# A decoder layer on one core: input loads held in program order, activation sums made in small steps, one input transposed two half-steps later

## The chip, the cores and the metric

The kernel runs on one core of a Trainium2 chip. The time is that of one execution on the device in microseconds (us), as the median of several runs. The five engines of the core take part as follows: TensorE multiplies and transposes (PE in the profile, its weight loads PEld), ScalarE (ACT) and VectorE (DVE) prepare operands and finish results, SyncE (SP) starts nearly all transfers, and GpSimd (POOL) does next to nothing here.

## The reference

One layer on x of 256 rows by 2048 columns, in float32:

- h = x + half FFN 1, where a half FFN is `0.5 * ((silu(gate) * up) @ w_down)` with `gate, up = split(rmsnorm(x) @ w_gate_up)`. The hidden width is 5632, so w_gate_up is 2048 x 11264 and w_down 5632 x 2048.
- Three mixers on rmsnorm(h) @ w_in (causal window means, attention with a forget gate, attention to 256 memory rows), each gated; their sum goes through w_out (2048 x 2048) and is added to h.
- A second half FFN with its own norm and weights is added to that; the sum is the output.

## The kernel before

**Products.** Every float32 operand is cut into a high part and the remainder; a product is three matmuls (high by high, high weight-remainder, remainder by high), each of 128 x 128 by 512 columns. ScalarE writes the high part of a weight tile (`wh`), VectorE the remainder (`wl`). The activations are the stationary side: a page of the transposed input holds two slices of 128 input columns for both halves of the rows, as high part and remainder. `to_lhs_part` (L189) makes such a page: four transposes on TensorE (L197), then ScalarE (L186) and VectorE (L187) cut what stands in PSUM.

**Two kinds of groups.** `mm_group` (L318) is the ordinary one: 512 output columns, all of the input. It loads weights in pieces of four slices (1 MB, L327) into a ring of three `raw` buffers, cuts half a piece at a time (L339, L340), and issues twelve matmuls for it (L346). Such a half is called a half-step here. `pair_group` (L245) does two blocks of 512 columns together, in eight units of two slices each. In units 0 to 2 seven products take the place of eight: VectorE forms sums of weights (`ta` L286, `tb` L291 and L292; their cut parts are `hah`, `hal`, `hbh`, `hbl`), and the stationary side needs sums of activation blocks, called `form`, one page for each of the three units. `form_page` (L212) makes one: VectorE adds high part and remainder (L216), forms four sums of 128 x 128 per slice (L218 to L221) and the remainder (L224), ScalarE the high part (L223). Units run in the order 3, 0, 4, 1, 5, 2, 6, 7.

**The sides of the work.** A queue `side` holds small jobs: transposes of a page (`prepare` for x, `to_lhs` for later inputs), loads of small parameters, empty steps (`pause`). `tick` takes one job from it behind each half-step of an ordinary group, and in a pair group only in the units behind the last one with seven products. The first group of FFN 1, `pa`, is an ordinary one with finer first loads (one slice, one, two, then four) and a hook: `before(k0)` (L503) loads the next columns of x ahead of the half-steps that need them. Behind it come `pb` (again ordinary) and ten pair groups, then w_down. FFN 2 has the same shape. In `ffn`, three calls of `form_page` stand between `pb` and the first pair group (L458); in the w_out section they stand between its two ordinary groups and its pair group (L902); the mixers have theirs in `side` already (L605). `residual`'s `cb` adds a result to the old stream and puts its transposes into `side`; thus w_out's columns 0 to 1023 become pages of x2 first, and columns 1024 to 2047, which the pair group makes, become its last four pages.

**What sets the order.** The program is written in Python, but `TileContext(schedule_with_timeline_sim=True)` (L945) arranges each engine's instructions anew by a timeline that it estimates itself. Only what is wrapped in `keep_in_program_order` keeps its place. Each engine runs its list strictly in that order, so an instruction that waits holds up all behind it. Transfers that SP starts share one queue.

Of the kernel before, what the change touches and what calls it, by code (L numbers as in the profile page):

```python
# [32 lines left out]
def hybrid_layer(  # L33
# [27 lines left out]
    nc = tc.nc  # L61
# [9 lines left out]
    side = deque()  # L71
    pause = [lambda: None]
# [10 lines left out]
    def page(shape, dtype, name):  # L83
        return pp.tile([P, *shape], dtype, tag="p", name=name)

    def pages(n, shape, dtype, name):
        return [page(shape, dtype, name) for _ in range(n)]

    def bank(name):
        return mp.tile([P, 512], F32, tag="m", name=name)  # L90

    def temp(shape, name, dtype=F32):
        return tp.tile([P, *shape], dtype, tag="t", name=name)
# [5 lines left out]
    xv = x[0].rearrange("(t p) d -> p t d", p=P)  # L99
    xc = pages(4, [T, 512], F32, "xc")  # L100

    def load_x(c0, n):
        nc.sync.dma_start(out=xc[c0 // 512][:, :, c0 % 512 : c0 % 512 + n], in_=xv[:, :, c0 : c0 + n])

    load_x(0, 256)
    rows0 = cp.tile([16, P], F32, name="rows0")
# [6 lines left out]
    for _ in range(2):  # L113
# [12 lines left out]
        out=tri, in_=tri, pattern=[[1, S]], compare_op=ALU.is_ge, fill=0.0, base=0, channel_multiplier=-1  # L126
# [4 lines left out]
        out=mask, in_=mask, pattern=[[-1, P]], compare_op=ALU.is_ge, fill=MASKED, base=0, channel_multiplier=1  # L131
# [77 lines left out]
    def lhs_of(tiles):  # L209
        return lambda k, part, t: tiles[k // 2][:, k % 2, part, t * P : (t + 1) * P]  # L210

    def form_page(forms, tiles, j):  # L212

        xp = tiles[j]
        v, f = temp([2, S], "fv"), temp([4, P], "ff")
        nc.vector.tensor_tensor(v, xp[:, :, 0, :].bitcast(F32), xp[:, :, 1, :].bitcast(F32), ALU.add)  # L216
        a12, a22, a11, a21 = (v[:, kk, t * P : (t + 1) * P] for kk in range(2) for t in range(T))
        nc.vector.tensor_tensor(f[:, 0, :], a21, a22, ALU.subtract)  # L218
        nc.vector.tensor_tensor(f[:, 1, :], f[:, 0, :], a11, ALU.subtract)
        nc.vector.tensor_tensor(f[:, 2, :], a11, a21, ALU.subtract)  # L220
        nc.vector.tensor_tensor(f[:, 3, :], f[:, 1, :], a12, ALU.add)  # L221
        dst = page([2, 4, P], F32R, "form")
        nc.scalar.activation(dst[:, 0, :, :], f, AF.Copy)  # L223
        nc.vector.tensor_tensor(dst[:, 1, :, :], f, dst[:, 0, :, :].bitcast(F32), ALU.subtract)  # L224
        forms.append(dst)
# [92 lines left out]
    def mm_group(w, c0, kt, lhs, cols=((0, 512),), before=None, need=None):  # L318

        ncol = sum(n for _, n in cols)  # L320
        per, half = 2048 // ncol, 1024 // ncol
        ps = [[bank("mm") for _ in cols] for _ in range(T)]
        cuts = [0, 1, 2, *range(4, kt + 1, per)] if before else [*range(0, kt, per), kt]
        for k0, k1 in zip(cuts, cuts[1:]):
            nk = k1 - k0
            raw = wp.tile([P, per, ncol], F32, tag="raw", name="raw")
            nc.sync.dma_start(  # L327
                out=raw[:, :nk, :],
                in_=w[k0 * P : (k0 + nk) * P, c0 : c0 + ncol].rearrange("(k p) c -> p k c", p=P),
            )  # L330
            if before:
                before(k0)
            if need:
                need(k0)
            for h0 in range(0, nk, half):
                nh = min(half, nk - h0)
                wh, wl = (b.rearrange("p (k c) -> p k c", c=ncol) for b in parts(half * ncol))
                rv, hv, lv = raw[:, h0 : h0 + nh, :], wh[:, :nh, :], wl[:, :nh, :]
                nc.scalar.activation(hv, rv, AF.Copy)  # L339
                nc.vector.tensor_tensor(lv, rv, hv.bitcast(F32), ALU.subtract)  # L340
                for t in range(T):
                    for kk in range(nh):
                        k = k0 + h0 + kk
                        for i, (o, n) in enumerate(cols):
                            for q, (part, wt) in enumerate(((0, wh), (0, wl), (1, wh))):
                                nc.tensor.matmul(  # L346
                                    ps[t][i][:, :n],
                                    lhs(k, part, t),
                                    wt[:, kk, o : o + n],
                                    start=k == 0 and q == 0,  # L350
                                    stop=k == kt - 1 and q == 2,
                                )
                tick()
        return ps
# [5 lines left out]
    def row_rstd(ss, name):  # L360
        r = st.tile([P, T], F32, tag="rr", name=name + "r")
        nc.vector.tensor_reduce(r, ss, axis=AX.X, op=ALU.add)
        return rsqrt(r, T, 1.0 / D, name)

    def sums(acc, terms, n):

        return [[acc[t, n]] + ([terms[t, n]] if terms else []) for t in range(T)]
# [34 lines left out]

        return cb, tiles, rs, Stream([kept[c].rearrange("p (t n) -> p t n", t=T) for c in range(4)])

    def ffn(lx, xt, rs, wgu, wd, stream, cb, before=None):

        hid, forms, flat = [], [], {}
        hdram = dp.tile([NFC - 1, P, 4 * S], F32, tag="hd", name="hd", bufs=2)
        rh = st.tile([P, T], F32, tag="rh", name="rh")

# [44 lines left out]
        pb = mm_group(wgu, FF, KD, lx)  # L455
        hd = gated(0, [pa[t][0] for t in range(T)], [pb[t][0] for t in range(T)])
        side.extend(put(0, hd))
        for j in range(3):  # L458
            form_page(forms, xt, j)
        for c in range(1, NFC):  # L460
            if c == NFC - 1:
                side.extend(put_last)
# [35 lines left out]
    tiles0, rs0 = [], []  # L498
# [16 lines left out]
    def row_sums(cs):  # L515
        for c in cs:
            for t in range(T):
                tc.keep_in_program_order(sumsq(ss0, t, c, xc[c][:, t, :]))
# [3 lines left out]
    for c in range(1, 4):  # L522
        side.append(lambda c=c: prepare(c, 0))
        side.append(lambda c=c: prepare(c, 1))
    side.append(lambda: row_sums(range(4)) or rs0.append(row_rstd(ss0, "x0")))
    side.append(small_loads)
    side.extend(pause * 6 + [small_cols])
    s0 = Stream([xv[:, :, c * 512 : (c + 1) * 512] for c in range(4)])
    cb, x1, rs, s1 = residual(s0, G_MIX, "x1", wait=3)
    lx = lhs_of(x1)  # L530
    ffn(lhs_of(tiles0), tiles0, rs0, ffn1_w_gate_up[0], ffn1_w_down[0], s0, cb, before=before)


    def head_norm(buf, nh, name):
# [67 lines left out]
                )  # L602

    forms1 = []
    side.extend(lambda j=j: form_page(forms1, x1, j) for j in range(3))  # L605
    side.append(load_mem)
    side.extend(pause)
    for c in range(4):
# [239 lines left out]
    mg = []  # L848
# [46 lines left out]

    cb, x2, rs, s2 = residual(s1, G_FFN2, "x2")
    lg = lhs_of(mg)
    for c in range(2):
        s1.load(c)
        ps = mm_group(w_out[0], c * 512, KD, lg)  # L900
        cb(c, [[ps[t][0]] for t in range(T)])
    formsg = []  # L902
    for j in range(3):
        form_page(formsg, mg, j)
    for c in range(2, 4):
        s1.load(c)
    po, terms = pair_group(w_out[0], 1024, 1536, lg, formsg, MIXED)
    for n in range(2):
        cb(2 + n, sums(po, terms, n))


    def store(c, ps):
# [1 line left out]
        for t in range(T):  # L914
            nc.sync.dma_start(out=out[0, t * P : (t + 1) * P, c * 512 : (c + 1) * 512], in_=o[:, t, :])

    ffn(lhs_of(x2), x2, rs, ffn2_w_gate_up[0], ffn2_w_down[0], s2, store)


# [30 lines left out]
```

## Time and profile before

| | |
|---|---|
| median of 3 runs | 2164.21 us (2162.13 to 2168.88) |
| the profiled execution | 2164.95 us, its span 2163.2 us |
| granted TensorE clock, mean | 0.997 of full speed |
| PE busy | 2142.4 us (99%), 9770 matmuls and transposes |
| PEld busy | 1764.5 us (82%) |
| DVE busy | 1572.2 us (73%) |
| ACT busy | 1136.0 us (53%) |
| DMA | 444.63 MB, mean 206 GB/s |

Busy time counts a matmul from its issue to its modelled end, and neighbours overlap; so 99% does not say that matmuls follow each other as closely as they can. How closely they do is read from a run of equal matmuls: its length over their number. The span is what the engines' records cover; the execution is 1.75 us longer.

### The profile page before, as it was taken

The numbers are of one execution on the slowest core, as the hardware profiler recorded it, in microseconds if no ns is written. First come the engines' busy times: TensorE is split into PE (matmuls) and PEld (weight loads), VectorE is DVE, ScalarE is ACT, GpSimd is POOL, SyncE is SP. The second block draws the span as 40 slices with busy tenths as digits, with TensorE's granted clock in tenths as the row PEclk, the third lists the DMA queues.
The fourth block names the chain that finished last, engine by engine and source line by source line (L and its number), as shares of the span: only waits on it lengthen the run. The fifth ranks groups of instructions, "written<-read, shape, count | busy, mean of one in ns | idle before, by whom it ended". The sixth has DMA issues, their size and how long they took to land.

```text
span 2163.2 us, 25670 instructions
## 1 busy us (share of the span) xinstructions
PE 2142.4 (99%) x9770; PEld 1764.5 (82%) x9770; DVE 1572.2 (73%) x1959; ACT 1136.0 (53%) x1412; POOL 3.5 (0%) x24
## 2 busy tenths in 40 slices
PE   8999999999999999999999999999999999999999
PEld 5888888888888888887788888878788888888887
DVE  4799889887554678657645777687989889984443
ACT  5455555556444465555644555455555555563332
POOL 0000000000000000000000000000000000000000
PEclk8999999999999999999999999999999999999999
DMA  6566666668666655754455656565666666686663
GB/s 215 175 220 219 213 206 212 215 212 304 212 205 207 236 182 158 242 172 149 144 194 192 196 180 217 193 222 183 211 217 215 220 207 214 205 311 233 204 200 112
DMA packets 219680, 444.63 MB, mean 206 GB/s; under 512 B 10831, under 2 KB 11941, under 8 KB 219557
## 3 DMA queue, kind: packets, MB, share of 16 engines
q1 hardware_dynamic: 219264, 442.95, 61.8%
q8 instruction: 76, 1.25, 0.2%
q14 instruction: 48, 0.39, 0.0%
q10 hardware_dynamic: 292, 0.05, 0.0%
HBM read 426.16 MB, written 16.79 MB: 205 GB/s over the span
## 4 chain that ended last, share of the span: by engine, by line
PE 94%; DVE 2%; DMA 2%; ACT 1%; issue 0%; SPq 0%; ACTq 0%
PE mm L346 48%; PE mm L241 42%; DMA raw<-in_ffn_w_gate_up_dram 2%; DVE wl L236 1%; PE hid L422 1%; ACT wh L235 0%; PE x L197 0%; DVE hal L236 0%; DMA xc<-in_x_dram 0%; PE fpt L829 0%; DMA raw<-in_w_out_dram 0%; PE fav L839 0%; ACT wh L339 0%; DVE tb L291 0%; DVE form L224 0%
## 5 line engine op out<-in xcount | busy, mean ns | idle before, releaser
L340 DVE TENSOR_TENSOR wl<-raw,wh 128x1024 fp32r<-128x1024 f32 (+2 forms) x393 | 471.0, 1200 | 405.8 <-ACT wh L339 405.0
L339 ACT ACTIVATE wh<-raw 128x1024 fp32r<-128x1024 f32 (+2 forms) x393 | 408.2, 1040 | 508.8 <-PE mm L346 447.9
L241 PE MATMUL mm<-wh,x 128*128 128x512 f32 x2116 | 655.0, 391 | 0.0
L235 ACT ACTIVATE wh<-raw 128x1024 fp32r<-128x1024 f32 (+1 forms) x384 | 374.4, 979 | 371.8 <-PE mm L241 188.2
L236 DVE TENSOR_TENSOR wl<-raw,wh 128x1024 fp32r<-128x1024 f32 (+1 forms) x384 | 424.6, 1118 | 101.3 <-ACT wh L235 99.7
L241 PEld LDWEIGHTS mm<-wh,x 128*128 128x128 f32 x2116 | 394.5, 188 | 80.7 <-ACT wh L235 0.3
L346 PE MATMUL mm<-wh,hid 128*128 128x512 f32 x1408 | 435.4, 390 | 0.0
L241 PE MATMUL mm<-wl,x 128*128 128x512 f32 x1058 | 408.2, 390 | 0.0
L346 PE MATMUL mm<-wh,x 128*128 128x512 f32 (+1 forms) x1216 | 375.6, 386 | 9.5 <-ACT x L186 8.1
L346 PEld LDWEIGHTS mm<-wh,hid 128*128 128x128 f32 x1408 | 264.3, 188 | 54.5
L346 PE MATMUL mm<-wl,hid 128*128 128x512 f32 x704 | 274.0, 389 | 0.0
L346 PEld LDWEIGHTS mm<-wh,x 128*128 128x128 f32 x1216 | 225.3, 189 | 58.1 <-ACT x L186 10.2
L241 PEld LDWEIGHTS mm<-wl,x 128*128 128x128 f32 x1058 | 198.6, 188 | 41.8
L346 PE MATMUL mm<-wl,x 128*128 128x512 f32 (+1 forms) x608 | 232.1, 382 | 0.0
L346 PEld LDWEIGHTS mm<-wl,hid 128*128 128x128 f32 x704 | 132.2, 188 | 27.4
L346 PEld LDWEIGHTS mm<-wl,x 128*128 128x128 f32 x608 | 115.2, 189 | 20.7 <-issue 0.3
L235 ACT ACTIVATE hbh<-tb 128x1024 fp32r<-128x1024 f32 x72 | 75.8, 1053 | 35.5 <-DVE tb L292 35.4
L286 DVE TENSOR_TENSOR ta<-raw 128x1024 f32<-128x1024 f32 x72 | 87.6, 1217 | 8.0 <-DMA raw<-in_ffn_w_gate_up_dram 7.0
L236 DVE TENSOR_TENSOR hbl<-tb,hbh 128x1024 fp32r<-128x1024 f32 x72 | 87.7, 1218 | 6.8 <-ACT hbh L235 6.8
L236 DVE TENSOR_TENSOR hal<-ta,hah 128x1024 fp32r<-128x1024 f32 x72 | 87.7, 1218 | 0.8 <-ACT hah L235 0.8
L241 PE MATMUL mm<-hah,form 128*128 128x512 f32 x288 | 86.0, 389 | 0.2 <-ACT hah L235 0.2
L235 ACT ACTIVATE hah<-ta 128x1024 fp32r<-128x1024 f32 x72 | 75.7, 1052 | 19.2 <-DVE ta L286 19.1
(319 smaller groups left out, 1923.2 us busy)
## 6 DMA issues: line engine op xcount, KB each, us to landing
raw<-in_ffn_w_gate_up_dram SPq DMA_DIRECT2D x321, 512.0 KB, 4.6
raw<-in_ffn_w_down_dram SPq DMA_DIRECT2D x88, 1024.0 KB, 5.2
raw<-in_w_in_dram SPq DMA_DIRECT2D x52, 1024.0 KB, 5.2
raw<-in_w_in_dram SPq DMA_DIRECT2D x48, 512.0 KB, 4.7
raw<-in_ffn_w_gate_up_dram SPq DMA_DIRECT2D x15, 1024.0 KB, 6.6
hd<-hf SPq DMA_DIRECT2D x20, 512.0 KB, 4.8
hg<-hd SPq DMA_DIRECT2D x20, 512.0 KB, 6.7
raw<-in_w_mem_kv_dram SPq DMA_DIRECT2D x8, 1024.0 KB, 7.7
```

The lines of the kernel that those rows point to most:

```text
L235: nc.scalar.activation(dst[0], src, AF.Copy)
L236: nc.vector.tensor_tensor(dst[1], src, dst[0].bitcast(F32), ALU.subtract)
L241: nc.tensor.matmul(ps, sides[part], wt[i][:, col : col + 512], start=start and q == 0, stop=stop and q == 2)
L286: nc.vector.tensor_tensor(ta, s[:, 3:4, :].to_broadcast([P, 2, 512]), s[:, 1:3, :], ALU.add)
L339: nc.scalar.activation(hv, rv, AF.Copy)
L340: nc.vector.tensor_tensor(lv, rv, hv.bitcast(F32), ALU.subtract)
L346: nc.tensor.matmul(ps[t][i][:, :n], lhs(k, part, t), wt[:, kk, o : o + n], start=k == 0 and q == 0, stop=k == kt - 1 and q == 2,)
L422: nc.tensor.transpose(ps[:, j, t * P : (t + 1) * P], hd[t][:, k * P : (k + 1) * P], ident)
```

## The change

Three edits. First, the loads of x and the weight loads of the group with a hook are wrapped in `keep_in_program_order`, so SP issues them as they are written. Second, `form_page` is no longer called between groups: `form_steps` puts its three calls into `side`, beside `pa` and `pb` of each FFN and beside the two ordinary groups of w_out; the empty steps ahead of `small_cols` go from 6 times `pause` to 3 times. Third, twice `pause` goes into `side` ahead of the last transposes of x2, which puts these two half-steps further into FFN 2's `pa`.

```diff
--- before.py
+++ after.py
@@ -100,7 +100,9 @@
     xc = pages(4, [T, 512], F32, "xc")
 
     def load_x(c0, n):
-        nc.sync.dma_start(out=xc[c0 // 512][:, :, c0 % 512 : c0 % 512 + n], in_=xv[:, :, c0 : c0 + n])
+        tc.keep_in_program_order(
+            nc.sync.dma_start(out=xc[c0 // 512][:, :, c0 % 512 : c0 % 512 + n], in_=xv[:, :, c0 : c0 + n])
+        )
 
     load_x(0, 256)
     rows0 = cp.tile([16, P], F32, name="rows0")
@@ -324,10 +326,12 @@
         for k0, k1 in zip(cuts, cuts[1:]):
             nk = k1 - k0
             raw = wp.tile([P, per, ncol], F32, tag="raw", name="raw")
-            nc.sync.dma_start(
+            load = nc.sync.dma_start(
                 out=raw[:, :nk, :],
                 in_=w[k0 * P : (k0 + nk) * P, c0 : c0 + ncol].rearrange("(k p) c -> p k c", p=P),
             )
+            if before:
+                tc.keep_in_program_order(load)
             if before:
                 before(k0)
             if need:
@@ -402,9 +406,11 @@
 
         return cb, tiles, rs, Stream([kept[c].rearrange("p (t n) -> p t n", t=T) for c in range(4)])
 
-    def ffn(lx, xt, rs, wgu, wd, stream, cb, before=None):
-
-        hid, forms, flat = [], [], {}
+    def form_steps(forms, tiles, n=3):
+        return [lambda j=j: form_page(forms, tiles, j) for j in range(n)]
+
+    def ffn(lx, forms, rs, wgu, wd, stream, cb, before=None):
+        hid, flat = [], {}
         hdram = dp.tile([NFC - 1, P, 4 * S], F32, tag="hd", name="hd", bufs=2)
         rh = st.tile([P, T], F32, tag="rh", name="rh")
 
@@ -455,8 +461,6 @@
         pb = mm_group(wgu, FF, KD, lx)
         hd = gated(0, [pa[t][0] for t in range(T)], [pb[t][0] for t in range(T)])
         side.extend(put(0, hd))
-        for j in range(3):
-            form_page(forms, xt, j)
         for c in range(1, NFC):
             if c == NFC - 1:
                 side.extend(put_last)
@@ -523,12 +527,14 @@
         side.append(lambda c=c: prepare(c, 0))
         side.append(lambda c=c: prepare(c, 1))
     side.append(lambda: row_sums(range(4)) or rs0.append(row_rstd(ss0, "x0")))
+    forms0 = []
+    side.extend(form_steps(forms0, tiles0))
     side.append(small_loads)
-    side.extend(pause * 6 + [small_cols])
+    side.extend(pause * 3 + [small_cols])
     s0 = Stream([xv[:, :, c * 512 : (c + 1) * 512] for c in range(4)])
     cb, x1, rs, s1 = residual(s0, G_MIX, "x1", wait=3)
     lx = lhs_of(x1)
-    ffn(lhs_of(tiles0), tiles0, rs0, ffn1_w_gate_up[0], ffn1_w_down[0], s0, cb, before=before)
+    ffn(lhs_of(tiles0), forms0, rs0, ffn1_w_gate_up[0], ffn1_w_down[0], s0, cb, before=before)
 
 
     def head_norm(buf, nh, name):
@@ -602,7 +608,7 @@
                 )
 
     forms1 = []
-    side.extend(lambda j=j: form_page(forms1, x1, j) for j in range(3))
+    side.extend(form_steps(forms1, x1))
     side.append(load_mem)
     side.extend(pause)
     for c in range(4):
@@ -895,18 +901,19 @@
 
     cb, x2, rs, s2 = residual(s1, G_FFN2, "x2")
     lg = lhs_of(mg)
+    formsg, forms2 = [], []
+    side.extend(form_steps(formsg, mg))
     for c in range(2):
         s1.load(c)
         ps = mm_group(w_out[0], c * 512, KD, lg)
         cb(c, [[ps[t][0]] for t in range(T)])
-    formsg = []
-    for j in range(3):
-        form_page(formsg, mg, j)
     for c in range(2, 4):
         s1.load(c)
     po, terms = pair_group(w_out[0], 1024, 1536, lg, formsg, MIXED)
+    side.extend(pause * 2)
     for n in range(2):
         cb(2 + n, sums(po, terms, n))
+    side.extend(form_steps(forms2, x2))
 
 
     def store(c, ps):
@@ -914,7 +921,7 @@
         for t in range(T):
             nc.sync.dma_start(out=out[0, t * P : (t + 1) * P, c * 512 : (c + 1) * 512], in_=o[:, t, :])
 
-    ffn(lhs_of(x2), x2, rs, ffn2_w_gate_up[0], ffn2_w_down[0], s2, store)
+    ffn(lhs_of(x2), forms2, rs, ffn2_w_gate_up[0], ffn2_w_down[0], s2, store)
 
 
 # ---- launch: one core; inputs and outputs as the reference has them ----
```

The edits move nothing between engines, but the order that comes out differs in many places. Below, stretches of each engine's list, of before and then of the changed kernel.

SP, the start of the program: `xc` is a load of x (256 columns, then twice that), `raw` one of weights. Before:

```order
L103 DMA xc<-in_x_dram 128x2x256
L327 DMA raw<-in_ffn_w_gate_up_dram 128x512
L103 DMA xc<-in_x_dram 128x2x256
L327 DMA raw<-in_ffn_w_gate_up_dram 128x512
L327 DMA raw<-in_ffn_w_gate_up_dram 128x2x512
L327 DMA raw<-in_ffn_w_gate_up_dram 128x4x512 x3
L103 DMA xc<-in_x_dram 128x2x512
L327 DMA raw<-in_ffn_w_gate_up_dram 128x4x512 x2
L103 DMA xc<-in_x_dram 128x2x512
L327 DMA raw<-in_ffn_w_gate_up_dram 128x4x512
L103 DMA xc<-in_x_dram 128x2x512
L327 DMA raw<-in_ffn_w_gate_up_dram 128x4x512
```

Changed:

```order
L104 DMA xc<-in_x_dram 128x2x256
L329 DMA raw<-in_ffn_w_gate_up_dram 128x512
L104 DMA xc<-in_x_dram 128x2x256
L329 DMA raw<-in_ffn_w_gate_up_dram 128x512
L104 DMA xc<-in_x_dram 128x2x512
L329 DMA raw<-in_ffn_w_gate_up_dram 128x2x512
L329 DMA raw<-in_ffn_w_gate_up_dram 128x4x512
L104 DMA xc<-in_x_dram 128x2x512
L329 DMA raw<-in_ffn_w_gate_up_dram 128x4x512
L104 DMA xc<-in_x_dram 128x2x512
L329 DMA raw<-in_ffn_w_gate_up_dram 128x4x512 x5
```

The third load of x (columns 512 to 1023) stands ahead of the two-slice weight load now, where it stood behind three four-slice loads; the fourth and fifth have moved forward too, and no load stands ahead of its place in the program.

ACT, the first transposed pages of x and the first weights of `pa`; `wh_166` is the first cut of the two-slice load, `wh_195` and `wh_221` are those of the next. `x0_121` and `x0_141` are the first two pages of x, `x0_182` and `x0_211` the next two. Before:

```order
L186 ACTIVATE x0_121<-x0_122,cols0_94 128x256
L339 ACTIVATE wh_166<-raw_164 128x1024
L148 DMA rows_110<-in_fox_k_norm_dram 1x64 x2
L186 ACTIVATE x0_121<-x0_122,cols0_94 128x256
L150 DMA rows_110<-in_mem_q_norm_dram 1x128
L150 DMA rows_110<-in_mem_k_norm_dram 1x128
L339 ACTIVATE wh_195<-raw_192 128x1024
L339 ACTIVATE wh_221<-raw_192 128x1024
L151 DMA bforget_109<-in_b_forget_dram 128x16
L186 ACTIVATE x0_141<-x0_142,cols0_94 128x256
L339 ACTIVATE wh_250<-raw_247 128x1024
L339 ACTIVATE wh_276<-raw_247 128x1024
```

Changed:

```order
L188 ACTIVATE x0_121<-x0_122,cols0_94 128x256
L150 DMA rows_110<-in_fox_k_norm_dram 1x64 x2
L188 ACTIVATE x0_121<-x0_122,cols0_94 128x256
L152 DMA rows_110<-in_mem_q_norm_dram 1x128
L152 DMA rows_110<-in_mem_k_norm_dram 1x128
L153 DMA bforget_109<-in_b_forget_dram 128x16
L188 ACTIVATE x0_141<-x0_142,cols0_94 128x256 x2
L188 ACTIVATE x0_182<-x0_183,cols0_94 128x256
L188 ACTIVATE x0_211<-x0_212,cols0_94 128x256
L343 ACTIVATE wh_166<-raw_164 128x1024
L188 ACTIVATE x0_182<-x0_183,cols0_94 128x256
L188 ACTIVATE x0_211<-x0_212,cols0_94 128x256
```

Where `wh_166`, `wh_195` and `wh_221` stood ahead of the last cut of page `x0_141` and others behind, that page and the first half of the next two now come ahead of `wh_166`.

PE, from w_out's pair group (L241) to FFN 2's `pa` (L346); `x2` are pages of its input, made by transposes from `xr`. Before:

```order
L241 MATMUL mm_11285<-hal_11429,form_11208 128x512
L241 MATMUL mm_11289<-hal_11429,form_11208 128x512
L197 MATMUL x2_11518<-ident_89,xr_11014 128x128 x4
L346 MATMUL mm_11599<-wh_11603,x2_11036 128x512
L346 MATMUL mm_11599<-wl_11604,x2_11036 128x512
L346 MATMUL mm_11599<-wh_11603,x2_11036 128x512 x2
L346 MATMUL mm_11599<-wl_11604,x2_11036 128x512
L346 MATMUL mm_11599<-wh_11603,x2_11036 128x512
L346 MATMUL mm_11599<-wh_11629,x2_11062 128x512
L241 MATMUL mm_11296<-hbh_11438,form_11208 128x512 x2
L241 MATMUL mm_11229<-hbh_11438,mg_10610 128x512 x2
L346 MATMUL mm_11599<-wl_11630,x2_11062 128x512
```

Changed, in `pa` (whose matmuls are L350 now, transposes L199):

```order
L350 MATMUL mm_11600<-wl_11638,x2_11491 128x512
L350 MATMUL mm_11600<-wh_11637,x2_11491 128x512
L199 MATMUL x2_11654<-ident_89,xr_11211 128x128 x4
L350 MATMUL mm_11599<-wh_11663,x2_11517 128x512
L350 MATMUL mm_11599<-wl_11664,x2_11517 128x512
L350 MATMUL mm_11599<-wh_11663,x2_11517 128x512 x2
L350 MATMUL mm_11599<-wl_11664,x2_11517 128x512
L350 MATMUL mm_11599<-wh_11663,x2_11517 128x512
L350 MATMUL mm_11600<-wh_11663,x2_11517 128x512
L350 MATMUL mm_11600<-wl_11664,x2_11517 128x512
L350 MATMUL mm_11600<-wh_11663,x2_11517 128x512 x2
L350 MATMUL mm_11600<-wl_11664,x2_11517 128x512
```

Before, matmuls and a transposed page of `pa` stood between two pieces of the pair group's third seven-product unit. In the changed kernel `pa` has 36 matmuls on pages that are there already, and the first transposes of x2's last four pages (`x2_11654`) stand behind these.

## Rows read from the trace of the kernel before

**Rows 1.** Waits: engine, line, what for: us in all, times, longest.

```profile
PE mm L346 <- ACT x L186: 8.1, 4, 2.7
PE mm L241 <- ACT hbh L235: 3.8, 2, 2.0
```

**Rows 2.** Chain of waits: the start and a steady group: start, us, what, count.

```profile
8.13 7.22 DMA raw<-in_ffn_w_gate_up_dram
28.68 6.28 DMA xc<-in_x_dram
...
363.99 38.82 PE mm L241 x171
```

**Rows 3.** Busy by stretch: us, PE, PEld, DVE, ACT, POOL (count), PEclk, DMA share, GB/s.

```profile
7.80:16.20 8.40, 5.42 (x22) 3.46 (x22) 5.07 (x7) 4.52 (x6) 0.00 (x0) 1.00 0.96 335
16.20:23.00 6.80, 5.50 (x18) 4.04 (x17) 3.77 (x4) 3.49 (x6) 0.00 (x0) 0.50 0.95 354
33.30:40.10 6.80, 6.22 (x18) 4.86 (x19) 4.64 (x21) 3.98 (x10) 0.00 (x0) 0.50 0.12 41
```

**Rows 4.** The same view, matmuls of line 346 alone (PE, PEld).

```profile
7.80:70.05 62.25, 50.32 (x192) 37.55 (x192) 0.89 0.61 211
```

**Rows 5.** The same view, transposes of line 197 alone (PE, PEld).

```profile
7.80:70.05 62.25, 5.48 (x28) 4.72 (x28) 0.89 0.61 211
1398.70:1460.00 61.30, 3.65 (x24) 2.83 (x24) 1.00 0.62 207
```

**Rows 6.** Timeline of the start: start, us, engine, what, idle before and releaser.

```profile
11.84 1.06 ACT L339 ACTIVATE wh<-raw 128x1024 fp32r<-128x1024 f32 x1 [2.35 <-DMA raw<-in_ffn_w_gate_up_dram]
...
13.75 0.45 ACT L186 ACTIVATE x<-x,cols 128x256 fp32r<-128x256 f32 x1
...
14.26 0.50 PE L346 MATMUL mm<-wh,x 128*128 128x512 f32 x1 [2.69 <-ACT x L186]
...
28.40 1.03 PE L197 MATMUL x<-ident,xc 128*128 128x128 f32 x8
...
32.01 0.50 PE L346 MATMUL mm<-wh,x 128*128 128x512 f32 x1 [2.57 <-ACT x L186]
```

**Rows 7.** Groups by shape, 0 to 70 us: busy, mean ns, idle before.

```profile
L340 DVE TENSOR_TENSOR wl<-raw,wh 128x1024 fp32r<-128x1024 f32 x15 | 18.1, 1224 | 21.6 <-ACT wh L339 21.6
...
L187 DVE SCALAR_TENSOR_TENSOR x<-x,cols,x 128x256 fp32r<-128x256 f32 x16 | 7.3, 478 | 0.3 <-ACT x L186 0.2
```

**Rows 8.** Busy by stretch, from the first matmuls to the last first-group weights.

```profile
7.50:25.50 18.00, 13.42 (x48) 9.31 (x49) 11.02 (x15) 9.15 (x14) 0.00 (x0) 0.81 0.96 344
```

**Rows 9.** Groups by shape, VectorE, 60 to 115 us, the activation sums.

```profile
L216 DVE TENSOR_TENSOR fv<-x 128x512 f32<-128x512 f32 x3 | 2.0, 682 | 0.0
...
L224 DVE TENSOR_TENSOR form<-ff,form 128x512 fp32r<-128x512 f32 x3 | 2.0, 678 | 0.0
...
L218 DVE TENSOR_TENSOR ff<-fv 128x128 f32<-128x128 f32 x3 | 0.8, 283 | 0.0
```

**Rows 10.** Timeline, TensorE, three later places.

```profile
109.89 0.73 PE L241 MATMUL mm<-hbh,form 128*128 128x512 f32 x2 [1.71 <-ACT hbh L235]
...
1441.01 0.47 PE L346 MATMUL mm<-wh,x 128*128 128x512 f32 x1 [0.90 <-DVE xr L383]
...
1532.09 0.74 PE L241 MATMUL mm<-hbh,form 128*128 128x512 f32 x2 [2.04 <-ACT hbh L235]
```

**Rows 11.** Busy by stretch, two later places.

```profile
1398.70:1460.00 61.30, 58.56 (x260) 46.08 (x259) 53.33 (x72) 34.36 (x48) 0.00 (x0) 1.00 0.62 207
1525.00:1535.00 10.00, 7.96 (x36) 6.22 (x36) 9.45 (x10) 5.99 (x8) 0.00 (x0) 1.00 0.77 255
```

**Rows 12.** Chain of waits, the w_out sums: the first and the last piece.

```profile
1399.52 0.68 DVE fv L216
...
1410.19 0.35 DVE form L224
```

**Rows 13.** DMA issues: what, queue, count, KB each, us from issue to landing.

```profile
raw<-in_ffn_w_gate_up_dram SPq DMA_DIRECT2D x321, 512.0 KB, 4.6
```

## The prediction

> **What bounds the kernel now.** I read the chain of waits first. Where it lies on TensorE in one long piece, the piece gives the pace: 171 matmuls in 38.82 us, 0.227 us each [rows 2]. The rest of the reading is to count the matmuls and transposes of a stretch, charge each at its pace, and take that from the length of the stretch; what is left was lost. The busy share can't show this, because a matmul that starts late still counts as busy. The steady groups lose nothing, so only stretches that lose can give anything back, and the edits touch three sorts.
>
> The start, 7.80 to 70.05 us: 192 matmuls [rows 4] at 0.227 are 43.6 us, 28 transposes [rows 5] at 0.13 (eight in 1.03 us [rows 6]) are 3.6, so of 62.25 us some 15.0 are lost. The table of waits has 8.1 us of TensorE waiting for ScalarE's cut of x [rows 1]; 1.5 of it lies ahead of 7.80, so 6.6 is in the stretch, as 2.69 before 14.26 us, 2.57 before 32.01 [rows 6] and one of 1.3. The clock gives the second part: from 16.20 to 23.00 and from 33.30 to 40.10 it was granted at 0.50, that is 1.2 instead of 2.4 GHz, with 5.50 and 6.22 us of busy time [rows 3]; about half of that, 5.9 us, is loss. The remaining 2.5 are short gaps, and a first matmul behind a wait that takes longer.
>
> Why does TensorE wait for so small a cut? ScalarE's list had the cuts of later weights ahead of it: `wh` stood idle 2.35 us for its load until 11.84, two such cuts ran 1.06 us each, and only then came the cut of x at 13.75 [rows 6]. The loads of x came late as well: the last was issued at 28.68 and took 6.28 us [rows 2], behind weight loads that wait for one of three `raw` buffers.
>
> The first pair group of each FFN loses once, before a product with `hbh`: 1.71 us before 109.89 and 2.04 before 1532.09 [rows 10]; these two are the 3.8 us of [rows 1]. From 1398.70 to 1460.00 there are 260 instructions, 24 of them transposes [rows 5, 11]: 236 x 0.227 + 24 x 0.13 = 56.7 us of 61.30, so 4.6 are lost. In 1525 to 1535, 36 instructions with four transposes should take 7.8 of 10.0, so 2.2 are lost [rows 11].
>
> **The change part by part.** The durations are those of the execution of 2164.95 us, 0.74 above the median; I subtract from the former, and 0.74 at the end.
>
> *The loads.* Nothing is added; five loads of x and the weights between them move. In the list of SP no load of x stands any longer behind a weight load of a later half-step; the one that waits longest for a `raw` buffer, the weights of slices 12 to 15, is now behind the last x. ScalarE's list follows: all of page `x0_141` and the first halves of the next two stand ahead of `wh_166`. I replayed the start by hand. It is the old one up to 11.2 us. Then eight transposes take 1.03 [rows 6], to 12.2. From the end of the first four, 11.7, ScalarE cuts two halves (0.45 each) and then `wh` (1.06) [rows 6], until 13.7: TensorE waits 1.5. It issues two matmuls and waits for the remainder, 1.22 on VectorE [rows 7], until 14.95: 0.8. Further on only one cut of x stands behind row sums, about 0.5. So 2.8 us of waits stay. For the clock I take one dip of half the old length, 1.7 lost, since the first wait is still there; the ends are 0 and the old 5.9. Lost after: 4.5; gain 15.0 - 4.5 = 10.5 us.
>
> Are the bytes there? The weights whose issue is at 8.13 land at 15.35 [rows 2], as the last of 3.67 MB counted from the first load in the old order. The new order's first 3.67 MB end with columns 1024 to 1535 of x, so these land at about 15.4 and are wanted at 17.6. At 344 GB/s [rows 8] back and forth from there: the first 512-column load of x at 9.3 (wanted 11.2), the two-slice weights 10.8 (12.65), the next weights 13.8 (14.6), those after 18.4 (20), the last x 19.9 (24). The thinnest margin is 0.8 us. The cost taken is 0.
>
> *The sums, FFN 1 and FFN 2.* A page is two steps of 0.68 us, four pairs of nothing bigger than 0.28, so 0.68 + 4 x 0.28 + 0.68 = 2.5 us on VectorE [rows 9]; three are 7.5 us. No work goes away. They stood between `pb` and the first pair group, ahead of the weight sums, when VectorE also has `ta`, `tb` and the remainders; VectorE was busy 9.45 of 10.0 us at the second place [rows 11]. Beside `pa` and `pb`, an ordinary half-step costs VectorE one remainder of 1.22 [rows 7] in 12 x 0.227 = 2.7 us of TensorE, so there is 1.5 us free in each: two half-steps hide a page, and the steps are spread one to a half-step, of which pages that are transposed at the same time take some. The two waits, 1.7 and 2.0 to 2.2, go. Should the cover fail, the same 7.5 us stands before the same group as now: bound 0 gain.
>
> *The sums of w_out.* The chain itself runs through them from 1399.52 to 1410.19 [rows 12], and VectorE is busy 53.33 of 61.30 us in this stretch [rows 11]. Three pages leave it for the two ordinary groups ahead. Of the 4.6 us I count 3.7 as gone together with the next edit; from none to all is the bound.
>
> *The transposes two half-steps later.* TensorE's list now has 36 matmuls of `pa` (8.2 us) ahead of the transposes of x2's last four pages. The wait that they answer, 0.90 for the added stream before 1441.01 [rows 10], goes. What is late next: those pages are wanted two half-steps of 2.7 us behind the first transposes, VectorE still has the pair group's end and two columns of added stream, and each page takes four steps, 0.45 on ScalarE and 0.48 on VectorE twice over [rows 6, 7]. I find about 1 us to spare. No row shows this order; the bounds are 0 and a return of the whole 4.6. I take about 1 us lost in all three later places together.
>
> Sum: 10.5 + (1.7 + 2.2 + 4.6 - 1.0) = 18.0; 2164.95 - 18.0 - 0.74 = 2146.2 us.
>
> **The rivals.**
>
> *A, the clock still falls.* The new first waits, 1.5 and 0.8, lie where the old ones did, just ahead of a stretch at 0.50 [rows 3]. If two dips come, 5.9 are lost instead of 1.7: 2150.4. For it: the clock had stayed at 1.00 from 7.80 to 16.20, although TensorE was busy only 5.42 of 8.40 us there [rows 3], and fell afterwards. Against it: the new waits are together half as long, and the second old dip came behind the wait before 32.01, which goes. The Trainium skill, "TensorE: Matmul & The Clock Gate", in "Part 1: The HAM clock gate (the "warmup" mystery)", says that the clock's default is half speed, that activity releases it, and that the monitor runs free, so that the same kernel can find its phase otherwise from run to run. The fall behind waits agrees with it; by that rule the gain hangs on phase as well as on waits.
>
> *B, x2's last pages come late.* Moving them shortens the time between transposing and use; if VectorE lags, TensorE waits for the remainder early in FFN 2 and the 4.6 us come back: 2150.8. For it VectorE's 53.33 of 61.30; against it the 7.5 us that leave.
>
> *C, the start is set by bytes, so the order doesn't do what it should.* DMA is 0.96 busy from 7.5 to 25.5 us [rows 8]. x ahead of weights then only exchanges a wait for x by one for weights; the margin of 0.8 us is soon used up. Then only the later 7.5 remain: 2156.7.
>
> *D, slower.* In the old order pieces of several units stand mixed in the first pair groups; in the new one each unit is finished before the next. A seven-product unit's weight sums can start only when its load has landed, 4.6 us behind the issue [rows 13], and the issue waits until VectorE releases one of three buffers. If VectorE enters these groups without a lead, two of the three units show a landing each, in three first groups: 3 x 2 x 4.6 = 27.6 us lost against 18.0 gained: 2173.8. It decides as soon as VectorE, now loaded with sums up to the end of the ordinary groups, is behind TensorE when the pair group begins. Against it: the later pair groups run unit by unit at 0.227 [rows 2].
>
> **How the numbers follow.** Forecast 0.60 (2141 to 2150), A 0.15 (2148 to 2153), B 0.10 (2148 to 2153), C 0.08 (2153 to 2160), D 0.07. The low end is the case that nothing is lost at all: 15.0 + 8.5 = 23.5 us, 2140.7. The range 2140 to 2156 leaves out D and most of C. A measurement of this kernel can tell 0.3%, 6.5 us, from no change, that is 2157.7: faster has the first three, 0.85, and half of C; the same has 0.05, slower D with some remainder, 0.06.
>
> **What would show it.** Right: TensorE's first wait behind 7.80 is some 1.5 us, for `wh`, near 12 to 14, and none for a cut of x longer than 1; the last x issued before 12 us; the first pair group beginning at 58 to 60 instead of 70; no wait for `hbh` above 0.5 in FFN 1's or FFN 2's first; the chain of w_out without sums. A shows as stretches at 0.50 between 12 and 45 us, B as a wait for a remainder of x2 early in FFN 2, C as waits for weight loads under 25 us, D as waits for loads in the first pair groups. I am wrong if the start still lasts past 66 us, or if what the three later places give is under 3 us.

## The result, and the profile after

The changed kernel takes 2143.65 us (median of 4 runs, 2142.92 to 2143.71) against 2165.15 (2162.13 to 2168.88): ratio 0.990, 95% interval 0.988 to 0.992. The profiled execution is 2142.92 us, span 2141.2, granted clock 1.000; before it was 2164.95. So 22.0 us went between the two profiled executions where the sum had 18.0, and the median lies 2.6 us under the forecast of 2146.2, inside the range. (A fourth run of the kernel before moved its median from 2164.21 to 2165.15.)

The start first. The first pair group begins at 58.25 us instead of 70.05: 11.8 us. The same stretches as in [rows 3], after (columns as there):

```profile
7.80:16.20 8.40, 6.27 (x32) 4.54 (x31) 4.70 (x9) 4.88 (x9) 0.00 (x0) 1.00 1.01 344
16.20:23.00 6.80, 6.80 (x36) 5.72 (x35) 5.90 (x8) 4.96 (x8) 0.00 (x0) 1.00 1.04 387
33.30:40.10 6.80, 6.80 (x31) 5.62 (x31) 6.80 (x14) 5.11 (x8) 0.00 (x0) 1.00 0.49 155
```

Between 7.80 and 16.20 there are 32 matmuls and transposes now, where there were 22, and the two other stretches are at full clock and full of work. What TensorE still waits for, in the table of waits (us in all, times, longest):

```profile
PE mm L350 <- ACT wh L343: 1.6, 1, 1.6
...
PE mm L350 <- ACT x L188: 1.3, 2, 1.0
PE mm L350 <- DVE wl L344: 0.5, 1, 0.5
```

The 8.1 us for cuts of x [rows 1] are 1.3, and the wait for `hbh` is gone from the list. The new first wait, in the timeline:

```profile
10.86 1.09 PE L199 MATMUL x<-ident,xc 128*128 128x128 f32 x8
...
11.55 0.91 ACT L188 ACTIVATE x<-x,cols 128x256 fp32r<-128x256 f32 x2 [0.91 <-PE x L199]
...
12.45 1.06 ACT L343 ACTIVATE wh<-raw 128x1024 fp32r<-128x1024 f32 x1
...
13.56 0.74 PE L350 MATMUL mm<-wh,x 128*128 128x512 f32 x2 [1.61 <-ACT wh L343]
...
14.82 0.50 PE L350 MATMUL mm<-wl,x 128*128 128x512 f32 x1 [0.52 <-DVE wl L344]
```

Eight transposes, two cuts of x on ScalarE, then `wh`, then the remainder: this is the chain replayed by hand, with 1.61 and 0.52 where it had 1.5 and 0.8.

In the chain of waits (start, us, what, count) the first pair group and the passage from w_out to FFN 2 are TensorE alone, piece joined to piece; `fv`, `form` and `wl` [rows 12] are not in it:

```profile
58.25 33.32 PE mm L243 x147
...
1384.75 33.33 PE mm L243 x147
1418.08 0.44 PE x L199 x4
1418.52 2.78 PE mm L243 x12
1421.30 0.44 PE x L199 x4
1421.74 5.49 PE mm L243 x24
1427.23 8.17 PE mm L350 x36
1435.40 0.44 PE x L199 x4
1435.83 2.75 PE mm L350 x12
1438.59 1.31 PE x L199 x12
1439.89 10.25 PE mm L350 x45
```

One can check the pace in it: 147 instructions in 33.32 us are 0.227 each. The later places gave 22.0 - 11.8 = 10.2 us. By the starts of such pieces in both chains, 2.3 of it lie in FFN 1's pair groups, 5.3 between w_down of FFN 1 and the first pair group of FFN 2, and 2.6 in FFN 2's pair groups.

### The profile page after: what moved, and what is told of

It reads as the page before. It is cut to its first block, busy times and chain, and to the rows that moved or that the text cites. A ratio compares the mean times of both kernels' runs of the same rounds, so it can differ in the third digit from the quotient of the medians.

```text
span 2141.2 us, 25671 instructions
## 1 busy us (share of the span) xinstructions
PE 2132.6 (100%) x9770; PEld 1761.2 (82%) x9770; DVE 1572.0 (73%) x1959; ACT 1135.9 (53%) x1412; POOL 3.5 (0%) x24
## 4 chain that ended last, share of the span: by engine, by line
PE 99%; DMA 1%; ACT 0%; issue 0%; DVE 0%; SPq 0%; ACTq 0%
PE mm L350 48%; PE mm L243 47%; PE hid L428 1%; DMA raw<-in_ffn_w_gate_up_dram 1%; PE x L199 0%; PE fpt L835 0%; PE fav L845 0%; ACT junk L362 0%; PE mg L199 0%; PE memT L199 0%; PE flg L807 0%; PE mav L740 0%; PE mlg L713 0%; PE flg L805 0%; PE fav L847 0%; PE fav L846 0%
## 5 line engine op out<-in xcount | busy, mean ns | idle before, releaser
L350 PE MATMUL mm<-wh,hid 128*128 128x512 f32 x1408 | 435.6, 390 | 0.0
L350 PE MATMUL mm<-wh,x 128*128 128x512 f32 (+1 forms) x1216 | 371.3, 383 | 2.9 <-ACT wh L343 1.6
L350 PEld LDWEIGHTS mm<-wh,hid 128*128 128x128 f32 x1408 | 264.3, 188 | 54.8
L350 PE MATMUL mm<-wl,hid 128*128 128x512 f32 x704 | 274.0, 389 | 0.0
L350 PEld LDWEIGHTS mm<-wh,x 128*128 128x128 f32 x1216 | 223.8, 188 | 48.4 <-issue 2.9
L350 PE MATMUL mm<-wl,x 128*128 128x512 f32 (+1 forms) x608 | 231.2, 381 | 0.5 <-DVE wl L344 0.5
L350 PEld LDWEIGHTS mm<-wl,hid 128*128 128x128 f32 x704 | 132.2, 188 | 27.2
L350 PEld LDWEIGHTS mm<-wl,x 128*128 128x128 f32 x608 | 114.3, 188 | 21.6 <-DVE wl L344 1.0
```

The source lines that it names most:

```text
L350: nc.tensor.matmul(ps[t][i][:, :n], lhs(k, part, t), wt[:, kk, o : o + n], start=k == 0 and q == 0, stop=k == kt - 1 and q == 2,)
```

## The experiments

**The first edit alone**, on the kernel before (the edits of this section are shown in outline):

```diff
+    tc.keep_in_program_order(<the loads of x>)
+    if before: tc.keep_in_program_order(load)
```

> The kernel before with the first edit alone: loads of x and of the first group's weights in program order. Theory (the edits add up; each acts at its own place): the whole start gain of 11 to 12 us and nothing else, about 2153.5 us; no stretch at half clock between 12 and 45 us, but the waits for hbh of 1.7 to 2.1 us in the first pair group of both FFNs and the losses around 1420 to 1440 us remain. Rival (the start gains only because sums leave VectorE's and ScalarE's lists there): under 6 us.

Measured: 2151.88 us against 2161.23 on the same chip, ratio 0.996 (0.994 to 0.997), 9.4 us faster. Its waits:

```profile
PE mm L243 <- ACT hbh L237: 2.8, 2, 1.4
PE mm L350 <- ACT x L188: 1.6, 1, 1.6
PE mm L350 <- ACT wh L343: 1.5, 1, 1.5
```

The waits for `hbh` are still there, the start has the shape of the changed kernel's: the first pair group begins at 59.02 us, where the kernel before had 70.05. The gain in the medians is 2 us short of the expected. The start has a stretch at half clock of its own, from 8.5 to 11.5 us, and the kernel before is faster on this chip, 2161.23 where the chip of the result had 2165.15. The rival is out.

**The second edit alone:**

```diff
-        for j in range(3): form_page(forms, xt, j)      # ffn, and w_out alike
+    side.extend(form_steps(forms, tiles))               # beside the ordinary groups
```

> The kernel before with the second edit alone: activation sums in steps beside the ordinary groups. Theory: the start is as slow as before (the first pair group begins near 70 us, half clock in it), the waits for hbh near 109 and 1530 us go (2.1 and 2.6 us lost there), and some 4 of the 5.4 us lost from 1400 to 1460 go: 8 to 9.5 us in all, about 2156 us. Rival (the later waits came from the late start and its order, not from the sums): within 2 us of before.

Measured: 2154.20 against 2161.23, ratio 0.997 (0.996 to 0.998), 7.0 us faster, 1 us under the lower end of what was expected. Its largest waits, without that for the warm-up's operand at the very start:

```profile
PE mm L346 <- ACT x L186: 10.1, 5, 5.1
...
PE x L197 <- DMA xc<-in_x_dram: 1.0, 1, 1.0
```

No wait for `hbh` and none for the added stream, while the cuts of x cost 10.1 us. So the later places are the sums' work, and the start is not. 9.4 + 7.0 = 16.4 of the some 17.6 us that both together gave on that chip (the experiment without the third edit, below).

The profiles say it place by place. The table has the start of a piece in each chain of waits (us):

| | FFN 1's first pair group | w_down of FFN 1 | FFN 2's first pair group | w_down of FFN 2 |
|---|---|---|---|---|
| before | 70.05 | 496.82 | 1492.02 | 1919.10 |
| first edit alone | 59.02 | 485.31 | 1479.55 | 1905.83 |
| second edit alone | 69.81 | 494.50 | 1484.47 | 1908.94 |
| changed | 58.25 | 482.72 | 1472.59 | 1897.07 |

Between the columns, the second edit alone takes 2.1, 5.2 and 2.6 us from the three later stretches and 0.2 from the start; the changed kernel takes 2.3, 5.3 and 2.6. The first edit alone takes 11.0 us from the start and 0.5, 1.0 and 0.8 from the rest. So the two edits account for two separate parts of the gain. (The profile of before is from another chip than the medians here, so its differences are larger than theirs.)

**The third edit alone, and the change without it:**

```diff
+    side.extend(pause * 2)     # alone, on the kernel before
-    side.extend(pause * 2)     # taken from the changed kernel
```

> The kernel before with the third edit alone: the last transposes of x2 two half-steps later. Theory: it can only take away the wait of about 1 us for the added stream near 1440 us, so 0 to 1.5 us: about 2164. Rival 1: it brings the whole 5.4 us of the stretch 1400 to 1460. Rival 2: without the sums moved it makes the pages of x2 late and costs 1 to 4 us.

> The changed kernel without the third edit. Theory: it loses 0 to 1.5 us against the changed kernel, at the entry of FFN 2 only: 2144 to 2145. Rival (the third edit carries the entry of FFN 2 and the sums alone don't): 3 to 5 us slower, about 2148.

Measured: alone 2161.68 against 2161.23, ratio 1.000 (0.999 to 1.001); the change without it 2143.64, as the changed kernel (2143.65, on another chip). In the kernel with the third edit alone the wait that it was to answer stands at 0.9 as before [rows 10]:

```profile
PE mm L241 <- ACT hbh L235: 2.8, 2, 1.4
...
PE mm L346 <- DVE xr L383: 0.9, 1, 0.9
```

It does nothing that this interval, 2 us either way, can tell. The 0.9 us went with the sums: the kernel with the second edit alone has no such wait.

**The changed kernel again, and the clock.** Three of the next kernels share a chip with a repeat of the changed kernel. In the first of them, the one with late cuts, ScalarE writes two first cuts three times, to make TensorE wait.

```diff
-                nc.scalar.activation(hv, rv, AF.Copy)
+                for _ in range(3 if before and k0 in (2, 4) and h0 == 0 else 1):
+                    nc.scalar.activation(hv, rv, AF.Copy)
```

> The changed kernel once more, to have it on the same chip as the next three: 2143 to 2144 us. Both theories of the clock expect the same start to show a stretch at half clock in some executions and none in others.

> The changed kernel with ScalarE's first cut of the two-slice weights and of the next weights each written three times instead of once, so that TensorE waits longer twice in the start: by the chain about 2.6 us more at the first, 1.2 at the second, 3.8 in all, 2147.4 us without any effect of the clock. Theory (the clock falls behind such waits, as in the kernel before): stretches at half clock behind them in most executions, 2 to 5 us more, 2149 to 2152 us. Rival (the clock falls by phase alone, whatever the waits): 2147 to 2148, half clock no more often than in the changed kernel.

Measured: 2144.14 (2143.50 to 2145.08) and 2147.75 (2147.52 to 2149.55). A stretch of the repeat, and one of the kernel with late cuts with the wait that it holds:

```profile
16.00:19.00 3.00, 3.00 (x9) 2.35 (x8) 2.21 (x2) 1.70 (x2) 0.00 (x0) 0.50 1.04 386
```

```profile
17.20:24.00 6.80, 4.76 (x15) 4.08 (x16) 2.86 (x6) 6.77 (x9) 0.00 (x0) 0.51 0.78 270
```

```profile
19.24 1.22 PE L351 MATMUL mm<-wh,x 128*128 128x512 f32 x2 [4.27 <-ACT wh L344]
```

The changed kernel had 1.00 throughout the start in its first profile and has 0.50 from 16 to 19 us in this one, with the same instructions; 3.00 us busy there at half speed is 1.5 lost. With late cuts the half-clock stretch is about twice as long, and all four executions have a mean granted clock of 0.998, where the four of the repeat have 0.999 to 1.000. The median is 3.6 us above the repeat's. By the profiles 2.1 of it are longer waits (4.27 against 1.65 and 0.53 in the repeat); that the 1.5 left are the clock's is an estimate, since the profiled execution is the slowest of the four. It also lost time ahead of the late cuts. From 8 to 13 us, in the kernel with late cuts and then in the repeat:

```profile
8.00:13.00 5.00, 5.00 (x14) 3.98 (x15) 1.93 (x5) 1.43 (x3) 0.00 (x0) 1.00 0.90 291
```

```profile
8.00:13.00 5.00, 4.23 (x24) 3.12 (x22) 2.46 (x6) 2.56 (x6) 0.00 (x0) 1.00 0.94 305
```

Single matmuls of the former take 0.63 us in the timeline there, as in the half-clock stretches, against 0.40 in the repeat, though the clock's column reads 1.00 in both: the pace of the instructions tells more than this column. The second wait that I expected did not come, and the number alone (2147.75) is inside the rival's range and under the theory's. The longer stretch and the clocks of the four executions speak for the theory, longer waits, longer half-clock stretches; with one profile of each kernel it isn't shown.

That the same instructions find half clock in one execution and none in another is shown by the repeat. The Trainium skill, "TensorE: Matmul & The Clock Gate", in "Part 1: The HAM clock gate (the "warmup" mystery)", says of the warm-up that the monitor runs free, so that the count of slow matmuls differs from run to run. The trace agrees, here for a fall in mid-work, with 3 us in one execution and 0 in the other.

Six more profiles of kernels with the new start have a clock of 0.50 from 8.60 to 11.60 us: the first edit alone, the change without the third, and below the small loads kept, the two with ScalarE's order and the doubled sums on the changed kernel. TensorE's first wait for a cut of x is 1.6 to 2.6 us long in these, and 1.0 and 1.5 in the two profiles of the changed kernel.

**What is left of the start.** In the trace after, the third load of x is issued only at 6.27 us, 3.5 us behind the one ahead of it; nothing on SP's list stands between them:

```profile
2.26 0.47 SPq L329 DMA_DIRECT2D raw<-in_ffn_w_gate_up_dram  x1
6.27 0.38 SPq L104 DMA_DIRECT2D xc<-in_x_dram  x1
6.69 1.31 SPq L329 DMA_DIRECT2D raw<-in_ffn_w_gate_up_dram  x2
```

In the order of instructions it waits for one of eight semaphores that this program's transfers take in turn, and that one is with a small parameter load, `pool_scale`, which ScalarE starts at 4.94 us behind its first cut. SP's table of waits says the same:

```profile
SPq L104 <- DMA rows<-in_pool_scale_dram: 3.5, 1, 3.5
```

The edit keeps these small loads where the program has them, later:

```diff
-            nc.scalar.dma_start(out=rows[...], in_=...)
+            tc.keep_in_program_order(nc.scalar.dma_start(out=rows[...], in_=...))
```

> The changed kernel with the eleven loads of small parameters kept at their place in the program too, behind the first group's work. In the changed kernel the 512-column load of x was issued only at 6.27 us, held by a semaphore that a small load had taken. Theory: it and the two-slice weights are issued before 3.5 us now, but nothing waits for them at 11 us, so the time changes by less than 0.5 us; the wait of 1.6 us for wh near 13 us stays. Rival 1 (the start waits for bytes): 1.5 to 2.5 us faster. Rival 2 (more transfers in flight delay the weights wanted first): 0.5 to 1.5 us slower.

Measured: 2144.02 against 2144.14, no difference. The loads do go out early, and by the semaphore updates in the traces the two-slice weights have landed at 10.62 us instead of 12.43:

```profile
2.27 0.47 SPq L329 DMA_DIRECT2D raw<-in_ffn_w_gate_up_dram  x1
2.78 0.55 SPq L104 DMA_DIRECT2D xc<-in_x_dram  x1
3.37 3.30 SPq L329 DMA_DIRECT2D raw<-in_ffn_w_gate_up_dram  x2
```

Then ScalarE's order, by keeping the cut of the two-slice weights and the cuts of the third and fourth page of x in program order; first with the small loads kept, then without:

```diff
+                if before and k0 == 2:
+                    tc.keep_in_program_order(cut_high)
+            if hold[0] and j0 == 0:          # pages 3 and 4 of x
+                tc.keep_in_program_order(part)
```

> As the kernel with the small loads kept, and ScalarE's cut wh of the two-slice weights kept ahead of the cuts of the third and fourth page of x. Theory (the 1.6 us that TensorE still waits near 13 us is ScalarE's order alone): the wait goes to under 0.3, the wait for the remainder behind it may stay at 0.5 to 0.7, 1.5 to 2 us faster than the changed kernel, about 2142. Rival (the wait only turns into one for the remainder or for the pages of x): less than 0.5 us.

> The changed kernel, its small loads where they were, with ScalarE's cut wh of the two-slice weights kept ahead of the cuts of the third and fourth page of x. Theory: the one-slice weights land as in the changed kernel again, 1 us sooner than in the kernel that kept both, and the wait of 1.6 us near 13 us goes, so 1.5 to 2.5 us faster than the changed kernel, 2141 to 2142.5 us. Rival (the two-slice weights, issued at 6.7 us, land only after 11.5): less than 1 us faster.

Measured: 2142.40 (2141.92 to 2142.96), 1.7 us under the repeat on the same chip, with ranges that do not touch; without the small loads kept 2143.27 (2142.80 to 2144.09), above the 2141 to 2142.5 expected, 0.9 us under the repeat, but on another chip and with a range that overlaps: inconclusive as a time. Profiles with half clock in the same place (8.60 to 11.60) compare more closely: the first pair group's first matmul begins at 59.17 us without the third edit and at 59.04 with the small loads kept, and at 57.97 and 57.90 with ScalarE's order, so the order is worth 1.1 to 1.2 us there. ScalarE and TensorE in the faster one:

```profile
7.43 0.63 ACT L346 ACTIVATE wh<-raw 128x512 fp32r<-128x512 f32 x1 [1.81 <-DMA raw<-in_ffn_w_gate_up_dram]
...
8.47 0.79 PE L355 MATMUL mm<-wh,x 128*128 128x512 f32 x1 [2.65 <-ACT x L189]
...
15.20 0.50 PE L355 MATMUL mm<-wl,x 128*128 128x512 f32 x1 [0.41 <-DVE wl L349]
```

The wait near 13 us is gone and 0.41 for the remainder stays, but the second weights were cut only at 7.43 (6.36 in the changed kernel, 6.60 in the repeat), and the first wait has grown to 2.65. Two loads issued behind these weights are in flight beside them now, but so they are with the small loads kept alone, where the cut came at 6.59; why it is so late here isn't shown. Without the small loads kept, ScalarE reaches `wh` early and stands:

```profile
12.45 1.06 ACT L346 ACTIVATE wh<-raw 128x1024 fp32r<-128x1024 f32 x1 [0.92 <-DMA raw<-in_ffn_w_gate_up_dram]
```

In the changed kernel's first profile the two-slice weights land at 12.43, just when ScalarE's two cuts of x are done: order and bytes end at the same time there. Where half clock delays the transposes, the cuts of x end later and the order counts. The kernel with both has the lowest median of all measured, 0.08% under the repeat on its chip.

**The sums made twice**, in the kernel before and in the changed one:

```diff
-    form_page(forms, tiles, j)
+    form_page([], tiles, j) or form_page(forms, tiles, j)
```

> The kernel before with every page of activation sums made twice at its place (the second copy is used, the first thrown away): 7.5 us more of VectorE between the groups, at each of FFN 1, w_out and FFN 2, and three more steps in the mixers' side queue. Theory (the later waits are VectorE's lead used up by work that stands ahead of the weight sums, and TensorE pays every further microsecond): 7 to 7.5 us more at each of the three places, 20 to 22 us, about 2184 us. Rival (the waits there are for the landing of weight loads, and the sums lie beside them): under 6 us in all.

> The changed kernel with every page of sums made twice in its step. The same 22 us of VectorE more, but beside half-steps of ordinary groups, each of which leaves VectorE 1.5 us of 2.7. Theory: hidden in FFN 1 and w_out; at the entry of FFN 2, where VectorE has the least room, 0 to 3 us; 2144 to 2147 us. Rival (the change hides the sums only just): 5 us or more.

Measured: on the kernel before 2195.57 against 2162.07, ratio 1.016 (1.014 to 1.017), 33.5 us slower, where 20 to 22 were expected; on the changed one 2151.93, about 8 us above its other medians, a number that was to speak for the rival. The three places in the former (columns as in [rows 3]):

```profile
85.00:140.00 55.00, 49.08 (x207) 37.19 (x207) 49.41 (x61) 30.02 (x36) 0.00 (x0) 1.00 0.54 182
1425.00:1480.00 55.00, 47.32 (x200) 35.07 (x199) 46.13 (x65) 27.82 (x34) 0.00 (x0) 1.00 0.57 191
1525.00:1580.00 55.00, 48.20 (x202) 35.88 (x201) 49.01 (x66) 30.38 (x35) 0.00 (x0) 1.00 0.53 182
```

At 0.227 each the 207, 200 and 202 instructions need at most 47.0, 45.4 and 45.9 of 55 us: at least 8.0, 9.6 and 9.1 are lost, where the account of before [rows 10, 11] had 1.7, 4.6 and 2.2. By the chains of the two profiles, which are 30.8 us apart, FFN 1's pair groups take 8.0 us longer, w_out with FFN 2's first two groups 7.1 and FFN 2's pair groups 7.9, for 7.5 us of added work each; the mixers take 8.4 longer. In the changed kernel TensorE's waits are those of the start and a single new one, none at FFN 1's first pair group, w_out or FFN 2:

```profile
PE memT L199 <- DMA mraw<-in_mem_dram: 5.8, 1, 5.8
```

That load of `mem` was issued at 750.26, in the changed kernel at 731.38:

```profile
750.26 2.00 SPq L605 DMA_DIRECT2D mraw<-in_mem_dram  x4
```

```profile
731.38 2.84 SPq L605 DMA_DIRECT2D mraw<-in_mem_dram  x4
```

In SP's list three more loads of weights stand ahead of it, and these waited, by SP's table from 735 to 752 us, for VectorE:

```profile
SPq L329 <- DVE ff L223: 8.5, 1, 8.5
SPq L268 <- DVE x1a L177: 4.4, 1, 4.4
SPq L329 <- DVE ff L221: 4.1, 1, 4.1
```

The clock falls during TensorE's wait and stays at half for some us behind it; half of the 3.95 us busy there is most of what is left of the 8:

```profile
752.70:759.40 6.70, 3.95 (x10) 3.21 (x11) 1.04 (x5) 2.02 (x7) 0.00 (x0) 0.50 1.00 375
```

The chain agrees: between w_down of FFN 1 and FFN 2's first pair group this kernel takes 7.9 us longer than the changed one, in both FFNs' pair groups nothing. The same wait, 5.9 us, is in the kernel before with doubled sums, and is part of its 33.5. So the theory holds at three places of both kernels, and the 8 us are a fourth mechanism, which neither theory had.

## Why the prediction was right, point by point

- *The start, 10.5 forecast, 11.8 found.* The mechanism is the one described: loads in order, so cuts of x ahead of cuts of weights. The waits left were 2.8 in the sum and are 1.61 + 0.52 + 0.3 = 2.4. The 1.7 for the clock wasn't lost in the profiled execution, which is luck: one such stretch stands in the repeat (1.5 lost) and in the six other profiles with 0.50 from 8.60 to 11.60 us. Two of them, rival A's 5.9, stand in none of these. In their place 0.8 us of short gaps were lost that the sum had at nothing. The first edit alone shows that the start is all the loads'. One sign was missed: the last load of x was issued at 12.66 us and not before 12.
- *The bytes.* The cost of 0 was right, its working was not. I had the two-slice weights land at 10.8; they land near 12.4, because their issue is held until 6.69; with the small loads kept early it isn't, and they land at 10.62. I counted bytes and not what SP waits for. It stayed without cost in the profiled execution only because ScalarE was busy with x until then. Rival C was nearer than its 0.08 for these weights, though not for the start as a whole.
- *The sums.* 1.7 + 2.2 + 4.6 were charged, 10.2 us found, as 2.3, 2.6 and 5.3: this is the term that was mis-sized, its mechanism is the one described. The pace account took 0.13 us for a transpose, from a row where eight stand alone, and the stretches were cut close around the waits. In the chain after, 36 matmuls and 4 transposes between 1427.23 and 1435.83 take 8.61, so a transpose is 0.11; for the 24 of the w_out stretch that makes 0.5 us of the 0.7 missing there.
- *One microsecond kept back* for new waits at the three places: none came. With the 1.7 of the sums and the 1.3 of the start (1.7 of the clock and 0.4 of the waits, less 0.8 of gaps) it makes the 4.0 us between 18.0 and 22.0.
- *The third edit* was credited with the 0.9 us at the entry of FFN 2. Wrong: alone it leaves that wait as it is, and rival B, which feared it, has nothing in the trace either.
- *Rival D* is out: the first pair groups run at 0.227 from their first matmul. VectorE enters them with its lead, and the doubled sums show that there was room for 7.5 us more.

## What to carry to other kernels

Count the instructions of a stretch at the pace of a steady one: what is left over is what can be won there, and it came out within 4 us of 22. Work for a helper engine that stands between two groups costs its full length once that engine's lead is used up (7.5 us more cost 7 to 8 here, at each of three places), and nothing when it is spread over stretches that leave it room. Before granting that a load is early enough, look at when it is issued and what its queue waits for, not only at the bytes ahead of it.

## What the runs showed of the hardware

- The spread of a kernel can be the clock's: on one chip the kernel before took 2158.99 to 2164.76 us with mean granted clocks between 0.999 and 0.996, the changed kernel without the third edit 2143.33 to 2144.10 with 0.999 to 1.000.
- A load whose place in its list is early can still be issued 3.5 us late: the transfers of this program take turns at eight semaphores, and a small parameter load of another engine held the one that was next. Keeping these small loads at their later place brought the issue from 6.27 to 2.78 us.
- Loads issued sooner may not be free: with two more in flight, the second 256 KB of weights were cut 1.67 and 2.44 us behind the first (the small loads kept, without and with ScalarE's order), where seven profiles of the new start with the later issue have 1.40 to 1.44.
- The granted clock's column can read 1.00 where matmuls run at the pace of half clock: from 8 to 13 us the kernel with late cuts had 14 instructions in 5.00 busy us, the repeat 24 in 4.23.
